# A trace-of-product kernel: four instead of two of the last batch's rows on TensorE, other last load groups, and two row tiles loaded as 96, 26 and 6 partitions

## The chip, the cores and the metric

The kernel runs on one core of a Trainium2 chip. The metric is device microseconds (us) of one execution; each kernel was executed several times, and the kernel before was executed beside it on the same chip. A profile gives the span from the first to the last instruction, some 1.8 us less than the metric.

## The reference

```python
B, N = 8, 2176
a, b = random (B, N, N) float32 each
prod = np.matmul(a, b)
return np.diagonal(prod, axis1=1, axis2=2).sum(axis=-1)   # 8 numbers
```

The trace of A·B is the sum over all i, k of A[i,k]·B[k,i]. No product matrix is needed: A must be transposed and multiplied with B element by element. Both inputs must be read once, 303 MB.

## The kernel before

GpSimd issues 55 of the 56 loads, all but the first, and the DMA turns float32 into bf16 on the way (the page has 303.04 MB read from HBM and 152.28 MB moved by the queues). A "row" below is a row tile: 128 rows of a matrix, 2176 wide, one row on each partition. For each batch, TensorE transposes A's row tiles, VectorE and ScalarE copy them out of the PSUM tiles `ps`, which TensorE's transposes write, into `at`, which holds the transposed A; VectorE then multiplies `at` with B's rows and sums:

```python
even = [ROWS] * (NT // ROWS) + [1] * (NT % ROWS)      # NT = 17, ROWS = 4
fine = [4, 4, 2, 2, 2, 2, 1]                          # B's load groups in the last batch
UNEVEN = ((0, 80), (80, 119), (119, P))               # P = 128
PE_ROWS = (13, 15)
LAST_PIECES = [(0, 2), (2, 3), (3, 5)]                # row 16, in units of 512 columns
...
def multiply_reduce(x, y, acc, out=None):             # VectorE
    nc.vector.tensor_tensor_reduce(
        out=x if out is None else out, in0=x, in1=y, scale=1.0, scalar=0.0,
        op0=MUL, op1=ADD, accum_out=acc,
    )
...
        if not last:
            for start, m, count in joined(b_groups):
                parts = UNEVEN if bi == BATCH // 2 and m == 1 else ((0, P),)
                groups, _ = load(b[bi], start, m, count, parts)   # one DMA for each part
                for start, m, b_t in groups:
                    on_dve(start // P, b_t)
```

In the last batch nothing is left to load behind B, so some of the work goes to TensorE: a row of PE_ROWS is 17 matmuls of 128x128 that add up in one PSUM tile, `trace_ps`, whose diagonal VectorE sums at the end (the closing reduction).

```python
                mine = [s for s in range(m) if v0 + s not in PE_ROWS]
                on_dve(v0 + mine[0], b_t[:, mine[0]:mine[-1] + 1, :])
                for s in range(m):
                    if s not in mine:
                        multiply_on_pe(at, b_t[:, s, :], v0 + s, 0, len(a_groups))
                continue
            ...                                        # row 16: three pieces, each shared by both
...
    with tc.issue_after(last_transpose.ins):
        for n, (x, y) in enumerate(pe_work):
            nc.tensor.matmul(
                trace_ps, x, y, start=(n == 0), stop=(n == len(pe_work) - 1),
            )
...
    multiply_reduce(tiles[f32], trace_ps, late_acc[:, cols:cols + 1], out=tiles["diagonal"])
```

## Time and profile before

| What | Before |
|---|---|
| Time, median of the three runs | 710.49 us |
| Share of 16 DMA engines' span, main queue | 100.2% |
| VectorE / ScalarE / TensorE busy | 57% / 28% / 27% |
| B loads landed, last batch: rows 8-9, 10-11, 12-13, 14-15 | 686.13, 691.25, 696.41, 702.24 |
| Row 16's pieces landed | 702.89, 703.50, 704.30 |
| The closing reduction starts | 705.93 |
| Span ends | 708.74 |

Read it from the bottom. From the closing reduction to the end are 2.8 us that no part of the change touches. Ahead of that, the last data lands at 704.30, and 1.63 us pass until the closing reduction. The 704 us before it are the DMA queue. A landing here is the time of the 16th semaphore step of a load, one step for each DMA engine, from the trace's semaphore events.

### The profile page before, as it was taken

How to read it: one execution, taken by the hardware profiler on the slowest of the kernel's cores; microseconds unless marked ns; L12 is line 12 of the kernel's file. 1: busy time of each engine (PE TensorE's matmuls, PEld its weight loads, DVE VectorE, ACT ScalarE, POOL GpSimd, SP SyncE). 2: the span in 40 equal slices, each digit the busy share in tenths (PEclk: the TensorE clock that was granted, in tenths of full speed). 3: DMA queues.
4: the chain of work that ended last, by engine and by line, in shares of the span. 5: the costliest groups of instructions: out<-in, count | busy, mean ns of one | idle time of the engine just before them, and what ended most of it. 6: DMA issues, size and time to landing. Idle time of an engine off the chain costs nothing.

```text
span 708.7 us, 3160 instructions
## 1 busy us (share of the span) xinstructions
PE 193.3 (27%) x1271; PEld 179.6 (25%) x1271; DVE 403.7 (57%) x204; ACT 197.2 (28%) x211; POOL 36.0 (5%) x63
## 2 busy tenths in 40 slices
PE   1542006420054100551006600056000670006703
PEld 0542005420054100550006500056000560005602
DVE  0223995138942389423893348933489335883398
ACT  2344005430064200652006510066000670006700
POOL 1000000000010000000001000000000000000100
PEclk9977556765577655776557765577655775557755
DMA  9999999999999999999999999999999999999997
GB/s 220 220 219 214 210 221 220 218 209 214 224 219 214 214 218 221 216 212 216 220 218 216 214 217 220 212 217 218 217 216 215 216 220 218 214 214 217 220 211 145
DMA packets 11681, 152.28 MB, mean 215 GB/s; under 512 B 914, under 2 KB 1170, under 8 KB 3090
## 3 DMA queue, kind: packets, MB, share of 16 engines
q0 software_dynamic: 11520, 150.97, 100.2%
q1 hardware_dynamic: 146, 1.11, 0.5%
q8 instruction: 10, 0.16, 0.1%
q14 instruction: 5, 0.04, 0.0%
HBM read 303.04 MB, written 0.00 MB: 428 GB/s over the span
## 4 chain that ended last, share of the span: by engine, by line
DMA 53%; DVE 27%; another core or an unknown queue 8%; issue 7%; PE 2%; ACT 1%; POOL 0%; DVEq 0%; POOLq 0%
DMA t<-in_b_dram 41%; DVE at L133 27%; DMA t<-in_a_dram 13%; PE ps L167 2%; ACT at L128 1%; POOL t L82 0%; DVE acc L133 0%; PE ps L188 0%; POOL identity masks.py:199 0%; DVE late L133 0%; DVE at L126 0%; DVEq L133 0%; POOL identity masks.py:197 0%; PE total L322 0%
## 5 line engine op out<-in xcount | busy, mean ns | idle before, releaser
L128 ACT COPY at<-ps 128x1024 bf16<-128x1024 bf16 x208 | 194.8, 1045 | 471.6 <-PE ps L167 471.4
L133 DVE CUSTOM_DVE_ANT_1 at<-at,t 128x8704 bf16<-128x8704 bf16 (+1 forms) x35 | 273.6, 7863 | 80.8 <-DMA t<-in_b_dram 80.8
L167 PE MATMUL ps<-identity,t 128*128 128x128 f32 x1088 | 179.3, 332 | 479.2 <-DMA t<-in_a_dram 468.5
L167 PEld LDWEIGHTS ps<-identity,t 128*128 128x128 f32 x1088 | 167.3, 212 | 488.1 <-issue 460.8
L126 DVE COPY at<-ps 128x1024 bf16<-128x1024 bf16 (+2 forms) x104 | 94.1, 907 | 215.4 <-PE ps L167 197.7
L82 POOL DMA_DIRECT2D t<-in_a_dram x23 | 15.4, 669 | 343.2 <-DVE acc L133 199.6
L133 DVE CUSTOM_DVE_ANT_1 at<-at,shared 128x8704 bf16<-128x8704 bf16 (+2 forms) x6 | 32.3, 5442 | 0.5 <-ACT at L128 0.5
L82 POOL DMA_DIRECT2D t<-in_b_dram x23 | 14.8, 646 | 238.8 <-PE ps L188 119.5
L188 PE MATMUL ps<-identity,t 128*128 128x128 bf16 x136 | 14.2, 219 | 5.0 <-DVE at L126 4.6
L188 PEld LDWEIGHTS <-t 128*128 128x128 bf16 x136 | 11.0, 100 | 8.4 <-issue 8.3
L307 PEld LDWEIGHTS <-at 128*128 128x128 bf16 x40 | 4.6, 123 | 28.9 <-issue 28.8
L307 PE MATMUL trace_ps<-shared,at 128*128 128x128 bf16 x32 | 4.0, 293 | 28.4 <-DMA shared<-in_b_dram 28.4
L82 POOL DMA_DIRECT2D shared<-in_b_dram x6 | 3.2, 534 | 55.1 <-PE ps L188 35.8
L101 DVE CAST t<-words 128x1088 bf16<-128x1088 f32 x1 | 0.7, 727 | 5.0 <-DMA words<-in_a_dram 5.0
L133 DVE DVE_READ_ACCUMULATOR2_ANT acc<- 128x1 f32 x35 | 2.9, 83 | 0.0
L100 ACT CAST t<-words 128x1088 bf16<-128x1088 f32 x1 | 1.1, 1099 | 3.8 <-DMA words<-in_a_dram 3.8
L292 POOL DMA_DIRECT2D b_t<-in_b_dram x3 | 1.6, 559 | 0.0
L100 ACT ACT_TABLE_LOAD x1 | 1.3, 1283 | 0.7 <-PEq L346 0.7
L133 DVE CUSTOM_DVE_ANT_1 at<-at,b_t 128x256 bf16<-128x256 bf16 (+1 forms) x3 | 1.4, 507 | 0.0
L265 DVE TENSOR_REDUCE sums<-acc 128x1 f32<-128x5 f32 x7 | 1.1, 157 | 0.2
L307 PE MATMUL trace_ps<-b_t,at 128*128 128x128 bf16 x8 | 1.1, 296 | 0.0
L133 DVE DVE_READ_ACCUMULATOR2_ANT late<- 128x1 f32 x10 | 0.8, 82 | 0.0
(18 smaller groups left out, 4.2 us busy)
## 6 DMA issues: line engine op xcount, KB each, us to landing
t<-in_a_dram POOLq DMA_DIRECT2D x16, 4352.0 KB, 45.5
t<-in_b_dram POOLq DMA_DIRECT2D x14, 4352.0 KB, 51.9
shared<-in_b_dram POOLq DMA_DIRECT2D x2, 2176.0 KB, 42.7
shared<-in_b_dram POOLq DMA_DIRECT2D x4, 1088.0 KB, 34.1
t<-in_a_dram POOLq DMA_DIRECT2D x7, 544.0 KB, 47.4
t<-in_b_dram POOLq DMA_DIRECT2D x6, 544.0 KB, 54.9
words<-in_a_dram SPq DMA_DIRECT2D x1, 1088.0 KB, 5.1
t<-in_b_dram POOLq DMA_DIRECT2D x1, 340.0 KB, 53.7
```

Of the source, the lines that this page charges most:

```text
L82: issued = nc.gpsimd.dma_start(out=part[lo:hi], in_=rows[lo:hi])
L100: nc.scalar.copy(out=t[:, 0, :half], in_=plain[:, :half])
L101: nc.vector.tensor_copy(out=t[:, 0, half:], in_=plain[:, half:])
L126: last_copy = nc.vector.tensor_copy(out=dst, in_=src)
L128: nc.scalar.copy(out=dst, in_=src)
L133: nc.vector.tensor_tensor_reduce(out=x if out is None else out, in0=x, in1=y, scale=1.0, scalar=0.0, op0=MUL, op1=ADD, accum_out=acc,)
L167: nc.tensor.transpose(ps[:, n * m + r, :], words[:, r, c0:c0 + step * (P - 1) + 1:step], tiles[f32],)
L188: last_transpose = nc.tensor.transpose(ps16[:, n, r, :], a_t[:, r, c0:c0 + P], tiles[bf16],)
L265: nc.vector.reduce_sum(out=tiles["sums"][:, bi:bi + 1], in_=acc[:, :cols], axis=mybir.AxisListType.X)
L292: loaded.append(nc.gpsimd.dma_start(out=row[:, lo:hi], in_=b[bi, start:start + P, lo:hi]))
L307: nc.tensor.matmul(trace_ps, x, y, start=(n == 0), stop=(n == len(pe_work) - 1),)
```

## The change

It has two unrelated intents. In the tail, two more rows move from VectorE to TensorE, and row 14 gets a load of its own, so that VectorE has no backlog when the last piece lands. In batches 3 and 5 (before: batch 4), B's single row is loaded in three parts, so that some of the 16 DMA engines get less work than the others and catch up. In the profile before, the semaphore steps ahead of the old split and behind it match within 0.01 us if three engines get 3 partitions less, nine get 1 more and four the same, at 0.325 us a partition.

```diff
-    fine = [4, 4, 2, 2, 2, 2, 1]
+    fine = [4, 4, 4, 2, 1, 1, 1]
-    UNEVEN = ((0, 80), (80, 119), (119, P))
-
-    PE_ROWS = (13, 15)
+    UNEVEN = ((0, 96), (96, 122), (122, P))
+    UNEVEN_BATCHES = (3, 5)
+
+    PE_ROWS = (11, 12, 13, 15)
...
-                parts = UNEVEN if bi == BATCH // 2 and m == 1 else ((0, P),)
+                parts = UNEVEN if bi in UNEVEN_BATCHES and m == 1 else ((0, P),)
...
-                on_dve(v0 + mine[0], b_t[:, mine[0]:mine[-1] + 1, :])
+                if mine:
+                    on_dve(v0 + mine[0], b_t[:, mine[0]:mine[-1] + 1, :])
```

## The prediction

> **What bounds it now.** I read the page's first three parts, then the chain of waits, the timeline of the last 40 us and, below the views, the packet and semaphore records of the trace.
>
> ```profile
> DVE  0223995138942389423893348933489335883398
> ...
> DMA  9999999999999999999999999999999999999997
> ...
> q0 software_dynamic: 11520, 150.97, 100.2%
> q1 hardware_dynamic: 146, 1.11, 0.5%
> q8 instruction: 10, 0.16, 0.1%
> ```
>
> All 16 DMA engines are busy in every slice but the last, and one queue fills 100.2% of their span: reading 303 MB is the bound. No other engine matters until the loads end. So the question is narrow: when does the last piece land, and what runs after it? The chain's last pieces (start us, us, what) and the timeline around them:
>
> ```profile
> 657.77 0.14 issue
> 657.90 6.11 PE ps L167 x28
> ...
> 664.04 8.35 ACT at L128 x9
> ...
> 672.42 8.54 DVE at L133
> ...
> 706.01 0.20 DVE diagonal L133
> ```
>
> ```profile
> 699.94 2.42 DVE L133 CUSTOM_DVE_ANT_1 at<-at,shared 128x2176 bf16<-128x2176 bf16 x1
> 702.28 2.01 PE L307 MATMUL trace_ps<-shared,at 128*128 128x128 bf16 x16 [3.59 <-DMA shared<-in_b_dram]
> ...
> 702.28 2.42 DVE L133 CUSTOM_DVE_ANT_1 at<-at,shared 128x2176 bf16<-128x2176 bf16 x1
> ...
> 704.33 1.11 PE L307 MATMUL trace_ps<-b_t,at 128*128 128x128 bf16 x8
> 704.63 0.69 DVE L133 CUSTOM_DVE_ANT_1 at<-at,b_t 128x512 bf16<-128x512 bf16 x1
> ...
> 705.26 0.40 PE L307 MATMUL trace_ps<-at,b_t 128*128 128x128 bf16 x1
> 705.59 0.42 DVE L133 CUSTOM_DVE_ANT_1 at<-at,b_t 128x256 bf16<-128x256 bf16 x1
> 705.93 0.28 DVE L133 CUSTOM_DVE_ANT_0 diagonal<-identity,trace_ps 128x128 bf16<-128x128 f32 x1
> ```
>
> The reader should see that VectorE (DVE) works without a pause from 672.42 to the last reduction at 705.93, and that TensorE (PE) ends its last row only at 705.66. The semaphore records put the landings of the last batch's B loads at 670.62, 680.91, 686.13, 691.25, 696.41, 702.24 (rows 14-15), then 702.89, 703.50 and 704.30 (three pieces of row 16). So after the last landing at 704.30 some 1.6 us pass until the closing reduction starts: that is what is left of VectorE's and TensorE's backlog, and it is all that a better tail can win. From 705.93 to the end, 708.7, nothing changes.
>
> [...]I sorted the 16 semaphore packets of the load ahead of the 80+39+9 split and of the load behind it and matched them; the shifts fit three engines 3 partitions short, nine with one more and four unchanged, to about 0.01 us, taking 0.325 us a partition (single rows take 2.6 us for 8). That is 5 each from the 80, 3 each on 13 engines from the 39, 1 each on 9 from the 9, both odd parts starting at the same engine. [...]ten 16384-byte instruction packets, about 0.96 us each, for TensorE's 2 x 1271 instructions; after each, one engine's semaphores are about 1.0 us late for good. So engines drift apart: at the last piece they end between 702.21 and 704.30, mean 703.69. [...]the granted clock is 0.50 after 674[...], and a row's 17 multiplications took 2.23 us in the tail (702.28 to 704.51).
>
> **The change, part by part.**
>
> *Rows to TensorE.* Rows 11 and 12 leave VectorE. A four-row reduction takes 9.22 us, two rows 4.68, one 2.42, so about 2.27 a row. VectorE's list becomes two of 9.22 from 672.42 (to 690.7), one of three rows, about 6.9 (to 697.7), row 14, then the row 16 pieces of 0.69, 0.42 and 0.42. Row 14 is now a load of its own: the bytes ahead of it land at 696.41 as before, plus 2.6 is 699.0, so it is done by about 701.4 instead of 704.63. VectorE then waits for the pieces and ends about 0.5 after the last lands. TensorE gets 4 rows of 2.2 us: row 11 lands with rows 8-11 at 691.25, rows 12-13 at 696.41 (4.4 us, to 700.8). Both fit in gaps in which it sat idle. Row 15 still lands with the sixteenth row's bytes, near 702, because the bytes ahead of it are the same. From there TensorE did 26 multiplications in 3.38 us (702.28 to 705.66), and this stays: TensorE becomes the last engine. The landing may improve: at 700.20 an instruction fetch held one engine, and rows 14-15 landed at 702.24, though the 15th of 16 engines was done at 701.59. The 51 extra pairs of TensorE instructions (34 multiplications for two rows, and 17 transposes, because each of the five A groups swaps one pair of rows for two single ones) bring the same block earlier, before row 15. I take 701.9 for it: 701.9 + 3.4 = 705.3, and the reduction at about 705.45 instead of 705.93. Win: **0.5 us**.[...]
>
> *Transposes.* A group of four A rows loses 4 fp32 transposes[...] and gains 8 bf16 ones[...]. Copies stay equal in number and size, 128x1024. They set the 672.42, so it stays.
>
> *The split.* Before: engines -3 (three), +1 (nine), 0 (four). By the same rule 96 gives 6 each, 26 gives 2 on 13 engines, 6 gives 1 on 6: -2 on three, +1 on six, twice over, so -4, +2, 0. Against before: three engines -1 (0.33 us earlier), six +1 (0.33 later), three -1 more, four unchanged. I followed each engine through the records: of the ten that end late (704.0 to 704.3), six are of the nine with +1. At most three of those get earlier, so some of the late ones end 0.1 to 0.3 us later. Cost: **0.2 us**, part of which also delays row 15 (already in 701.9).
>
> *Issue.* Two more loads on GpSimd, 0.54 us each, with 20 to 50 us from issue to landing: hidden. An extra 4-byte semaphore packet takes 0.02 us an engine: about 0.04 in all.
>
> Sum: -0.5 from the backlog and some 0.05 for packets; the 0.2 costs nothing more while TensorE, not the landing, ends last. 710.49 - 0.45 is about **710.0**.
>
> **Rivals.** (a) Balance decides: the new split meets the late engines better than I traced, the last landing moves to the mean, 703.7, and with the backlog gone the win is over 1 us: about 709.2. For it: the spread of 2.1 us is real and the change was made for it. Against: the fetches hit particular engines, and none of the late six can gain but three. (b) TensorE overfills: four rows at half clock are 8.9 us, and if rows 12-13 finish after row 15 lands, the end moves out: 711. Against: 700.8 is a full microsecond before 701.9. (c) All of it is hidden: 710.5, if row 15 lands at 702.3 again and TensorE ends at 705.7. (d) The third shared buffer, or the semaphores of the extra loads, delays an issue. Against: the last rows were issued at 670.7 with 20 us of loads queued ahead.
>
> **Range.** [...]the main line 710.0, (c) 710.5, (b) 711. The three runs before lie within 0.34 us, and the fetch hits could differ. So 709.2 to 710.8. Two per cent is 14 us, which no tail of 4.4 us after the last landing can give: within 2% at 0.98.
>
> **What would show it.** The last landing at 704.4 to 704.6; VectorE idle ahead of row 14 and ahead of row 16's pieces; TensorE working from 691, 696.5 and 701.9; the closing reduction waiting for TensorE; queue 0 still about 100%. It is wrong if the landings end before 704.1 or after 704.8, if a fetch still falls on row 15, if the granted clock is 1.0 at the end, or if loads in batches 3 or 5 leave a gap in the DMA row.

Cut beside the sum are a branch in which a higher granted clock speeds up row 15's matmuls (a win of up to 1.0 us, the author's estimate) and its place in the range; the range's low end, 709.2, is still rival (a)'s. What the trace of the kernel before shows of the clock: in each of the 15 bursts of transposes from 47 us on, it rises to 1.00 between 2.9 and 6.0 us after the first matmul, and it is back at 0.50 10 to 14 us after the rise. The float32 transposes start 0.213 us apart at 0.50 and 0.120 us at 1.00; the matmuls of `trace_ps` ran at 0.50 only. The copies out of `ps` number 208 on ScalarE and 104 on VectorE on both pages, before and after.

Two things rest on less than the text says. Which part of the 80+39+9 split falls on which engine is read from the shifts of the 16 steps, and the shares of the 96+26+6 split are an estimate from that reading. And that the ten packets of 16384 bytes belong to TensorE's instructions, 2 x 1271 on the page, so about 254 to a packet, and that 51 more pairs bring the last one earlier, was an estimate from these counts; the runs below agree with it: 51 spare matmuls moved the last packet from 700.2 to 674.2, and with 77 in the changed kernel there are eleven packets instead of ten.

## The result, and the profile after

The changed kernel took 710.01 us (median of six runs, 709.85 to 710.20) beside 710.47 (six runs, 710.38 to 710.72): 0.46 us less, and no run of one overlaps the other's. The ratio is 0.9993 with a 95% interval of 0.998 to 1.0006.

The chain of waits of the changed kernel, its last pieces (start us, us, what):

```profile
671.42 30.31 DMA shared<-in_b_dram
701.73 0.04 issue
701.77 3.39 PE trace_ps L309 x26
...
705.31 0.29 DVE diagonal L134
```

Before, this chain ran over VectorE from 672 on. Now it goes from a landing (row 15, at 701.73) to 26 matmuls on TensorE to the closing reduction. From 671 on VectorE is gone from the chain, up to the reduction itself. The timeline of the changed kernel shows it at work (the bracket is the idle time before an instruction and what ended it):

```profile
691.50 6.96 DVE L134 CUSTOM_DVE_ANT_1 at<-at,shared 128x6528 bf16<-128x6528 bf16 x1 [1.08 <-DMA shared<-in_b_dram]
...
699.26 2.42 DVE L134 CUSTOM_DVE_ANT_1 at<-at,shared 128x2176 bf16<-128x2176 bf16 x1 [0.79 <-DMA shared<-in_b_dram]
...
701.77 2.01 PE L309 MATMUL trace_ps<-shared,at 128*128 128x128 bf16 x16 [0.91 <-DMA shared<-in_b_dram]
...
703.00 0.69 DVE L134 CUSTOM_DVE_ANT_1 at<-at,b_t 128x512 bf16<-128x512 bf16 x1 [1.31 <-DMA b_t<-in_b_dram]
...
704.46 0.43 DVE L134 CUSTOM_DVE_ANT_1 at<-at,b_t 128x256 bf16<-128x256 bf16 x1 [0.38 <-DMA b_t<-in_b_dram]
...
704.75 0.40 PE L309 MATMUL trace_ps<-at,b_t 128*128 128x128 bf16 x1
...
705.31 0.29 DVE L134 CUSTOM_DVE_ANT_0 diagonal<-identity,trace_ps 128x128 bf16<-128x128 f32 x1 [0.41 <-PE trace_ps L309]
```

Every instruction of VectorE that is shown now has a wait in front of it, each ended by a landing, and the closing reduction waits 0.41 us for TensorE. Before, the corresponding lines had no brackets. The DMA part of the page is as before but for the packets of the two extra loads:

```profile
q0 software_dynamic: 11568, 150.97, 100.2%
```

The span splits into three terms. The first is the last landing; it went from 704.30 to 704.44. The second is the time from there to the closing reduction; it went from 1.63 to 0.87 us. The third, from the reduction to the end, is 2.8 us in both. The sum is -0.63 us in the two profiled executions (708.74 to 708.11), against -0.46 between the medians.

One more view is used below. The 16 semaphore steps of one load show how far the DMA engines have drifted apart. For the last piece of row 16 they ran from 702.21 to 704.30 before and from 701.77 to 704.44 after, with the same mean (703.69 and 703.72). So the drift has grown from 2.1 to 2.7 us: the new split moved work off engines that were ahead as well as off slow ones. The trace shows it. Of the 16 steps, batch 3's split relieves the tenth, fifteenth and sixteenth, but batch 5's relieves the first, seventh and eighth, and the last three keep all their work (the steps ahead of each split and behind it match within 0.01 us). Over the profiles below the drift is 2.0 to 2.3 us in the four with the old split and 2.5 to 3.0 in the eight with the new one, leaving out the fetch-late run.

### The profile page after: what moved, and what is told of

It reads as the page before. It is cut to its first block, busy times and chain, and to the rows that moved or that the text cites. A ratio compares the mean times of both kernels' runs of the same rounds, so it can differ in the third digit from the quotient of the medians.

```text
span 708.1 us, 3260 instructions
## 1 busy us (share of the span) xinstructions
PE 194.7 (27%) x1322; PEld 180.6 (26%) x1322; DVE 399.7 (56%) x200; ACT 196.6 (28%) x211; POOL 37.2 (5%) x65
## 4 chain that ended last, share of the span: by engine, by line
DMA 58%; DVE 24%; another core or an unknown queue 8%; issue 6%; PE 2%; ACT 1%; POOL 1%; DVEq 0%; POOLq 0%
DMA t<-in_b_dram 41%; DVE at L134 23%; DMA t<-in_a_dram 13%; DMA shared<-in_b_dram 4%; PE ps L168 2%; ACT at L129 1%; DVE at L127 1%; PE trace_ps L309 0%; POOL t L83 0%; PE ps L189 0%; POOL shared L83 0%; DVE acc L134 0%; POOL identity masks.py:199 0%; DVEq L134 0%
## 5 line engine op out<-in xcount | busy, mean ns | idle before, releaser
L168 PE MATMUL ps<-identity,t 128*128 128x128 f32 x1071 | 174.5, 328 | 481.5 <-DMA t<-in_a_dram 470.6
L168 PEld LDWEIGHTS ps<-identity,t 128*128 128x128 f32 x1071 | 162.3, 212 | 490.9 <-issue 462.8
L134 DVE CUSTOM_DVE_ANT_1 at<-at,shared 128x8704 bf16<-128x8704 bf16 (+2 forms) x4 | 27.8, 6957 | 1.9 <-DMA shared<-in_b_dram 1.9
L189 PE MATMUL ps<-identity,t 128*128 128x128 bf16 x170 | 16.4, 219 | 5.3 <-DVE at L127 4.9
L189 PEld LDWEIGHTS <-t 128*128 128x128 bf16 x170 | 13.0, 100 | 8.6 <-issue 8.4
L309 PEld LDWEIGHTS <-at 128*128 128x128 bf16 x72 | 8.4, 123 | 24.7 <-issue 24.5
L309 PE MATMUL trace_ps<-shared,at 128*128 128x128 bf16 x64 | 8.1, 294 | 23.8 <-DMA shared<-in_b_dram 23.8
L309 PE MATMUL trace_ps<-at,shared 128*128 128x128 bf16 x4 | 1.6, 396 | 0.0
```

What stands on the lines that cost most here:

```text
L134: nc.vector.tensor_tensor_reduce(out=x if out is None else out, in0=x, in1=y, scale=1.0, scalar=0.0, op0=MUL, op1=ADD, accum_out=acc,)
L168: nc.tensor.transpose(ps[:, n * m + r, :], words[:, r, c0:c0 + step * (P - 1) + 1:step], tiles[f32],)
L189: last_transpose = nc.tensor.transpose(ps16[:, n, r, :], a_t[:, r, c0:c0 + P], tiles[bf16],)
L309: nc.tensor.matmul(trace_ps, x, y, start=(n == 0), stop=(n == len(pe_work) - 1),)
```

## The experiments

The theory: the win is the backlog behind the last landing, the new split gives a little of it back, and the balance of the DMA engines is moved by instruction fetches that hit single engines (behind a fetch, one of the 16 steps comes 1.08 to 1.14 us later). Twelve kernels ran, in three jobs, each with five timed runs. "Backlog" is the time from the last landing to the closing reduction, in the one profiled execution. The intervals of two alone leave out 1: groups only (1.0001 to 1.0026) and the last one. So the readings below rest on profiles of one execution each, with medians beside them.

| Kernel | Median, us | Before, same job | Last landing | Backlog |
|---|---|---|---|---|
| before | 710.47 | - | 704.30 | 1.63 |
| the change | 710.01 | 710.47 | 704.44 | 0.87 |
| tail only | 709.79 | 710.36 | 704.30 | 0.88 |
| split only | 710.32 | 710.36 | 704.60 | 1.13 |
| no split | 710.66 | 710.36 | 705.09 | 0.93 |
| groups only | 711.40 | 710.36 | 704.50 | 2.22 |
| rows only | 710.63 | 711.07 | 704.63 | 0.94 |
| fetch early | 711.05 | 711.07 | 704.34 | 1.13 |
| fetch late | 711.25 | 711.07 | 705.78 | 0.89 |
| warm | 710.76 | 711.07 | 704.47 | 0.87 |
| half of row 15 | 709.91 | 710.43 | 704.70 | 0.81 |
| four pieces | 710.08 | 710.43 | 704.47 | 0.84 |
| both | 709.89 | 710.43 | 704.73 | 0.61 |
| both, old split | 709.61 | 710.43 | 704.43 | 0.62 |

In all 14 profiles the time from the closing reduction to the end of the span is 2.78 to 2.81 us, so landing and backlog are the whole story. In the second job (rows only to warm) the runs of every kernel, the one before too, scatter from 709.9 to 711.6; there, medians decide nothing below 1 us, and the profiles are read instead.

### The tail alone

```diff
-    UNEVEN = ((0, 96), (96, 122), (122, P))
-    UNEVEN_BATCHES = (3, 5)
+    UNEVEN = ((0, 80), (80, 119), (119, P))
+    UNEVEN_BATCHES = (4,)
```

> The new tail with the old 80+39+9 split in batch 4. Theory (the win is the backlog of VectorE after the last landing; the new split costs about 0.14 us of landing): 709.85 us, between 709.7 and 710.0, last landing near 704.30, closing reduction waiting for TensorE. Rival (the new split is what gains): 710.4.

It took 709.79 us (before 710.36). The last landing is at 704.30 as before, the backlog 0.88 as in the change. The tail carries the whole win. By the medians it is 0.57 us without the new split and 0.46 with it, but the runs of the two kernels overlap (709.74 to 710.24 and 709.85 to 710.20).

### The split alone

The kernel before with the new row split in batches 3 and 5:

```diff
-    UNEVEN = ((0, 80), (80, 119), (119, P))
+    UNEVEN = ((0, 96), (96, 122), (122, P))
-                parts = UNEVEN if bi == BATCH // 2 and m == 1 else ((0, P),)
+                parts = UNEVEN if bi in (3, 5) and m == 1 else ((0, P),)
```

> The old tail with the two 96+26+6 splits. Theory: 710.5 us, between 710.4 and 710.7; the last landing 0.1 to 0.2 later than 704.30, the first engine about 0.4 earlier, VectorE busy without a pause to the closing reduction near 706.0. Rival (the split gains): 710.0.

710.32 us (before 710.36): no win. The last landing is 704.60, 0.3 later than before, more than expected. The backlog is smaller than in the profile before, 1.13 against 1.63, though the tail is the same. VectorE's first reduction of the tail began at 671.88 here and at 672.42 in the profile before; over the 14 profiles it began between 671.81 and 672.70. What moves it was not tested. The old tail passes most of this scatter on to the end: behind the start VectorE waited only once here, 0.24 us for rows 4 to 7, which the expectation ("without a pause") did not have.

### No split

```diff
-    UNEVEN_BATCHES = (3, 5)
+    UNEVEN_BATCHES = ()
```

> The changed kernel with no row tile split at all. Theory (three engines owe their place to the split, and one of them took two instruction fetches): the slowest engine about 0.9 us later than with the old split, last landing near 705.2, 710.7 us. Rival (balance does not matter, the split is hidden): 710.0.

710.66 us, the last landing at 705.09 with a mean of 703.62: two engines end at 705.0 and 705.1, the other fourteen by 704.0. By these profiles a split is worth 0.5 to 0.8 us of landing, and the medians agree in sign: 0.30 us above the kernel before of the same job. Balance is not hidden; it is only that the new split does this job slightly worse than the old one.

### The groups alone

This run and the next are the changed kernel with one edit, so they keep the new split.

```diff
-    PE_ROWS = (11, 12, 13, 15)
+    PE_ROWS = (13, 15)
```

> The new groups, but rows 11 and 12 back on VectorE. Theory: VectorE has 9.2 us for rows 8-11 from 691.5, 2.4 each for rows 12 and 14 and 1.5 for the pieces, so it ends near 706.8 and the kernel takes 711.5 us. Rival (the row 14 load of its own is what gains): 710.0.

711.40 us. The timeline of VectorE in this kernel:

```profile
700.72 2.42 DVE L134 CUSTOM_DVE_ANT_1 at<-at,shared 128x2176 bf16<-128x2176 bf16 x1
...
706.37 0.42 DVE L134 CUSTOM_DVE_ANT_1 at<-at,b_t 128x256 bf16<-128x256 bf16 x1
...
706.72 0.28 DVE L134 CUSTOM_DVE_ANT_0 diagonal<-identity,trace_ps 128x128 bf16<-128x128 f32 x1
```

With four rows in one load, VectorE can start rows 8 to 11 only at 691.57, and without the help of TensorE it never catches up: no line here has a wait in front. The new groups alone make the kernel 1.0 us slower than before; the two rows on TensorE pay for that.

### The rows alone

```diff
-    fine = [4, 4, 4, 2, 1, 1, 1]
+    fine = [4, 4, 2, 2, 2, 2, 1]
```

> Four rows on TensorE with the old groups, so row 14 lands together with row 15. Theory: row 14 starts on VectorE at about 701.8 instead of 699.3, ends at 704.1, the pieces at 705.6, so 0.3 later than the changed kernel: 710.3 us. Rival (only the rows matter): 710.0.

The median, 710.63, is from the scattered job (before 711.07). In the profile row 14 starts at 701.92 on VectorE, as expected, and the closing reduction at 705.57, 0.26 later than in the change; but 0.19 of that is the last landing (704.63), and the backlog is 0.94 against 0.87. So the rows on TensorE make nearly all of the win, and row 14's own load adds under 0.1 us to it in this profile.

### The instruction fetch moved early

The kernel before, with 51 spare matmuls right behind the last transposes:

```diff
     with tc.issue_after(last_transpose.ins):
+        for _ in range(51):
+            nc.tensor.matmul(spare, tiles[bf16], tiles[bf16], start=True, stop=True)
```

> The kernel before with 51 spare matmuls on TensorE right behind the last transposes, which move the last instruction fetch from 700.2 to about 674, as in the changed kernel. Theory: rows 14-15 land near 701.6 instead of 702.24, but VectorE is busy to 702.3 either way, so 710.45 us, unchanged. Rival (the moved fetch is the win): 710.0.

711.05 us beside 711.07: no win by the medians. The last fetch moved to 674.2, and rows 14-15 landed at 701.63 instead of 702.24, both as expected; VectorE was busy to 701.81 and started row 14 then. The closing reduction came at 705.47, 0.46 earlier than in the profile before, which the expectation did not have: VectorE had begun the tail at 671.81, 0.61 earlier, and went through it without a pause. The fetch came after that start, so it did not cause it; and an earlier landing of row 14 gains nothing while VectorE is busy with rows before it.

### The instruction fetch moved late

The changed kernel with 77 such spare matmuls, so that one more fetch falls near the end:

```diff
+        for _ in range(77):
+            nc.tensor.matmul(spare, tiles[bf16], tiles[bf16], start=True, stop=True)
```

> The changed kernel with 77 spare matmuls right behind the last transposes: with them its instruction count behind the last fetch is what it was before, so another fetch comes near 700. Theory: row 15 lands up to 0.6 later than 701.73, TensorE is done 3.4 us after that, 710.5 us (710.1 if the fetch hits an engine that is ahead). Rival (the fetch is hidden): 710.0.

711.25 us (before 711.07, in the scattered job, so the medians decide nothing; but its fastest run, 710.71, is behind the fastest of the other kernels of this job, 709.91 to 710.13). In the profile it is slower, but by another way than expected. The extra fetch came at 701.4, too late for row 15. The fetch ahead of it, at 674.5, hit the engine that was already last: at the load of rows 4-7 its step came at 682.40, where the change has 681.06, while the first engine's was at 678.42 against 678.44. That engine kept the loss:

```profile
672.18 30.90 DMA shared<-in_b_dram
703.08 0.04 issue
703.12 3.40 PE trace_ps L312 x26
...
706.66 0.29 DVE diagonal L134
```

This is the chain of the change, 1.35 us later, with the same 3.4 us of TensorE. In the change, a fetch at nearly the same time, 674.0, hit an engine that was ahead of most (the third of 16), and cost nothing. Which engine a fetch hits is thus worth up to 1.3 us, more than the whole change. This may make the scatter of the second job. Only one execution of each kernel was profiled, so that stays open, and so does whether the spare matmuls or chance chose the engine that was hit here.

### TensorE's clock

The changed kernel with spare matmuls in TensorE's gaps, behind row 11 and behind row 13:

```diff
         for n, (x, y) in enumerate(pe_work):
+            if n in (17, 51):
+                for _ in range(24 if n == 17 else 10):
+                    nc.tensor.matmul(spare, tiles[bf16], tiles[bf16], start=True, stop=True)
```

> The changed kernel with 24 spare matmuls behind row 11 and 10 behind row 13, to fill TensorE's gaps and wake its clock. Theory: granted clock 1.0 from about 698, [...]and the end set by the last landing alone, the closing reduction near 705.05: 709.75 us. Rival (the landing sets the end already): 710.0.

The median is 710.76 in the scattered job (before 711.07); the backlog, 0.87, is exactly that of the change. The clock did rise. This is the window of rows 12 and 13 with the granted clock in the third column from the right (first the warm kernel, whose window also holds 25 other matmuls, then the change):

```profile
694.50:701.10 6.60, 5.86 (x59) 5.18 (x57) 5.80 (x3) 0.00 (x0) 0.00 (x0) 1.00 1.02 205
```

```profile
696.50:700.90 4.40, 4.31 (x34) 3.95 (x34) 3.61 (x3) 0.00 (x0) 0.00 (x0) 0.50 1.04 208
```

The timeline has the 34 matmuls of rows 12 and 13 from 696.57 to 700.88 in the first and from 696.55 to 700.87 in the second: 4.31 and 4.32 us at a clock of 1.00 and of 0.50. The edit did not fill the second gap: all 34 spare matmuls ran ahead of rows 12 and 13,

```profile
693.25 2.59 PE L312 MATMUL spare<-identity 128*128 128x128 bf16 x34
```

and the clock of the warm kernel was back at 0.50 for row 15. The kernel with the tail alone filled that in by chance: its clock was 1.00 from 700.4 to 703.8, and row 15's burst of 26 took 3.4 us all the same. So the granted clock does not set the pace of these matmuls. It does set that of the spare ones, whose operands are read without strides: their starts were 0.107 us apart at 0.50 and 0.056 us at 1.00, in the same run. What holds the others at about 0.12 us was not tested; one operand of each is read with a stride, which no run took away.

### Two limits that end together

TensorE's last matmul begins at 704.75 in the change, 25 matmuls of 0.119 us after the first, back to back; and the last landing, 704.44, plus three matmuls, gives nearly the same time (in the next run the last matmul begins 0.25 us after the landing, which would be 704.69 here). To tell these apart, the first 1024 columns of row 15 went to VectorE, which waits there:

```diff
-                        multiply_on_pe(at, b_t[:, s, :], v0 + s, 0, len(a_groups))
+                        g0 = 2 if v0 + s == 15 else 0
+                        multiply_on_pe(at, b_t[:, s, :], v0 + s, g0, len(a_groups))
+                        if g0:
+                            late.append((words_at(at, v0 + s, 0, g0), words_of(b_t[:, s, :], 0, g0)))
```

> The changed kernel with the first 1024 columns of row 15 on VectorE, which waits there anyway; TensorE has 18 instead of 26 multiplications behind row 15's landing. Theory (TensorE's backlog and the last landing end at the same time, within 0.1 us): TensorE now pauses ahead of the last piece, and the closing reduction comes only 0.0 to 0.1 earlier after the last landing: span minus last landing 3.6 instead of 3.66, 709.95 us. Rival (TensorE's backlog alone sets the end): 0.7 us earlier.

709.91 us; the backlog is 0.81. TensorE now pauses ahead of the last piece:

```profile
703.28 1.04 PE L312 MATMUL trace_ps<-b_t,at 128*128 128x128 bf16 x6
704.74 0.39 PE L312 MATMUL trace_ps<-b_t,at 128*128 128x128 bf16 x2 [0.41 <-DMA b_t<-in_b_dram]
```

The other limit alone, one matmul instead of three behind the last landing:

```diff
-    LAST_PIECES = [(0, 2), (2, 3), (3, 5)]
+    LAST_PIECES = [(0, 2), (2, 3), (3, 4), (4, 5)]
```

> The changed kernel with row 16 in four pieces, the last of 128 columns, so that one matmul is left behind the last landing instead of three. Theory: TensorE's 26 multiplications from row 15's landing still take 3.4 us, so no change, span minus last landing 3.6 to 3.7, 710.0 us. Rival (the last landing alone sets the end): 0.25 earlier.

710.08 us, the backlog 0.84: TensorE's 26 matmuls still take from 701.76 to 705.14. Then both edits together:

> Both edits together. Theory (two limits that end together, so only both edits win): span minus last landing 3.4, 709.75 us. Rival: as the better one of the two alone.

709.89 us, the backlog 0.61. TensorE ends with this:

```profile
704.57 0.39 PE L312 MATMUL trace_ps<-b_t,at 128*128 128x128 bf16 x2 [0.26 <-DMA b_t<-in_b_dram]
704.78 0.40 PE L312 MATMUL trace_ps<-at,b_t 128*128 128x128 bf16 x1
```

Two of its last three matmuls now belong to the piece before the last. Each edit alone took 0.03 to 0.06 off the backlog, both took 0.26 (four profiles with the tail of the change, the change, tail only, fetch late and warm, have backlogs of 0.87 to 0.89): the change had left two limits that end within 0.1 us of each other. The last landing happened to be 704.73 in this execution and ate the gain. With the old split instead of the new one:

```diff
-    UNEVEN = ((0, 96), (96, 122), (122, P))
-    UNEVEN_BATCHES = (3, 5)
+    UNEVEN = ((0, 80), (80, 119), (119, P))
+    UNEVEN_BATCHES = (4,)
```

> Both edits, and the old 80+39+9 split in batch 4. Theory: last landing 0.1 to 0.15 earlier than with the new split, unless the instruction fetches hit other engines; 709.6 us, the fastest of all. Rival (the split makes no difference): as the run with both edits.

709.61 us (709.53 to 709.93) beside 710.43 for the kernel before: a ratio of 0.9987, interval 0.9974 to 0.9999. It has the lowest median of all and is the only one whose interval was below 1. The backlog is 0.62, the landing 704.43.

## Why the prediction was right

The time was foretold as 710.0 and measured as 710.01. That is closer than the working deserves; term by term:

- **VectorE leaves the end, TensorE becomes last.** Shown by the chain of the change, and by the groups-only run, where VectorE keeps the end and the kernel takes 711.40. The terms held: three rows took 6.96 us (foretold 6.9), row 14 landed at 699.13 (699.0), row 15 landed at 701.73 (701.9), and its 26 matmuls took 3.39 us (3.38). VectorE did wait for rows 8 to 11, 1.08 us, which the list of its work had left out; nothing came of it, because there was slack behind.
- **The size of the win.** The closing reduction came 0.62 us earlier where 0.48 was foretold, and the medians moved by 0.46. The step "They set the 672.42, so it stays" was wrong: this start scatters by 0.9 us over the 14 profiles, and still by 0.54 over five kernels that are the same up to there (the change, warm, half of row 15, four pieces, both). The profile before was neither the earliest nor the latest, so one pair of profiles can't size this term to 0.1 us.
- **The split costs a little.** The shares read from the old split fit the change's first split too: matching the steps ahead of it and behind it gives three engines -2, six +1 and seven 0 to 0.01 us. The last landing, foretold 0.2 later, was 0.14 later. Over the eight profiles with the new split, leaving out the fetch-late one, it is 704.57 in the mean, over the four with the old split 704.34: 0.23. That it "costs nothing more" holds only because a part without a size was already in the 701.9 for row 15: row 15 waits for the same slow engines (701.73, and 701.60 in the tail-only run), and the last landing alone would have ended within 0.1 us of TensorE, so both limits move together. The medians of the tail-only run and of the last run point the same way, but within the overlap of the runs.
- **The last fetch moved.** It came at 674.0 instead of 700.2, and row 15 landed at 701.73, near the 701.9 that was worked out. Nearly the whole win passes through this landing: TensorE, now the last engine, starts row 15 0.51 us earlier (702.28 to 701.77) and ends 0.50 us earlier (705.66 to 705.16). With the old landing some 0.1 us would be left (an estimate: 705.66 and the 0.15 from TensorE's end to the reduction, against 705.93); that is rival (c). So the win needs both, VectorE out of the way and row 15 early. That the moved fetch is what made it early is likely but not shown: the fetch-early run speaks for it (rows 14-15 landed at 701.63), the split-only run against it (701.88, with its fetch at 700.28). No run has the new tail with a fetch on row 15; the fetch-late run was meant for that and missed. The size was a little off: matching the 16 steps ahead of a fetch and behind it gives one engine 1.08 to 1.14 us late, where the prediction has about 1.0. The fetch-late run shows what the prediction had only named as a risk, "the fetch hits could differ": one hit on the last engine undoes the win.
- **The clock.** The branch for a higher clock was wrong, though it moved no number: with the clock at 1.00 the matmuls of rows 12 and 13 kept their pace (34 in 4.31 us, against 4.32 at 0.50).

Of the rivals, (a), balance, is refuted by the split-only run, (b) by the 0.9 us that TensorE sat idle ahead of row 15, (c) by the medians and by row 15's landing, and (d) by the loads of the tail, which landed within 0.15 us of before.

## What to carry to other kernels

When a queue of loads bounds a kernel, split its end into three terms, last landing, backlog behind it and fixed ending, and work out what each engine still has to do when the last byte lands: the backlog is what moving work won here (1.63 to 0.87 us). Moving it also moved TensorE's last instruction fetch (700.2 to 674.0), and with the fetch a landing may shift (rows 14-15 landed at 702.24 with the fetch at 700.2, at 701.63 with it at 674.2), so look where the fetches fall. Check whether a second engine ends at nearly the same time, because then each edit alone looks useless (0.03 and 0.06 us of backlog here, against 0.26 for both). And look at the first and the last of the 16 semaphore steps of one load: where they drift apart by microseconds (2.0 to 3.0 in twelve of the profiles above), the last landing depends on the history of the late engines and not on the bytes alone (704.30 to 705.78 over these 14 profiles, for the same 303 MB).
